# Token groups of 768 and 512 instead of 640 and 640, with weights taken in quarters of a channel pair

## The chip, the cores and the metric

The kernel runs on one core of one Trainium2 chip. The metric is the device time of one execution in microseconds (us); smaller is better. Before the change the median of 3 runs is 2741.11 us (2739.73 to 2746.38). Engines are written as the profile writes them: PE is the matrix engine (its weight loads are PEld), DVE the vector engine, ACT the scalar engine, POOL GpSimd, and SP the engine whose queue issues every DMA of this kernel.

## What is computed

One encoder layer for 1280 tokens (1024 of a prompt and 256 of a sample) of width 2048, in float32:

```
hn   = rmsnorm(x, norm_w)
proj = einsum('btd,dp->btp', hn, w_in)            # 2048 -> 9232 columns
na_q, na_k, na_v, na_g, ml_qk, ml_v, ml_o, ml_z, ml_gp = split(proj)
att  = neighbourhood_attention(na_q, na_k, na_v, rpb) * silu(na_g)      # 8 heads of 128
qk   = silu(centred_depthwise_conv(ml_qk))
h    = rmsnorm(bidirectional_mlstm(mq, mk, ml_v, gates)) # 4 heads of 256
mem  = h * sigmoid(ml_o) * silu(ml_z)
y    = rmsnorm(x + concat(att, mem) @ w_out)             # 2048 -> 2048
```

## The kernel before, in words

A float32 product is made of three matmuls of a rounded type: every operand is split into a high and a low part (ACT casts the high part, DVE subtracts it to get the low part; `split`, L137, and `split_a`, L145), and high x high, high x low and low x high are added in PSUM (`mm_c`, L171). A weight block of 128 x 128 is the stationary operand, tokens are the moving one; for the values (`proj_v`) it is the other way round.

The 1280 tokens are cut into two groups of 640 (`GRP`, L20), and the program has five stages.

1. `first_tiles` (L175) loads group A's activations x, scales and splits them, makes sums and differences of the four blocks that two halves of the 2048 inputs (k tiles 0 to 7 and 8 to 15) and two halves of the tokens (`HALF` = 320) form, keeps them in SBUF (`xb`, `xg`) and computes the first 4 of 56 channel blocks of 128 in the plain way: 384 matmuls of 320 columns. `x_square` and `x_stats` (L117, L124) make the norm's factors.
2. `pair_a` (L236), 34 times: two channel blocks of group A at a time by seven products instead of eight (a 2 x 2 scheme over halves of the inputs and of the tokens). Each half `hf` of the k tiles loads four weight pieces of 128 x 512 (`ra`, 8 buffers), POOL makes four sums of them (`summed`, L278, tile `wt`, 4 buffers), ACT and DVE split the seven weights (`wsa`, 5 buffers), and PE runs 12 matmuls of 320 columns for each: 168 for a pair. In the second half `fold` (L250) adds the seven results from PSUM into `Cn` with eight additions on DVE (L248) and a copy on ACT, and `scaled` (L244) multiplies by the norm's factor. The last 8 pairs are values: PE transposes the result (L310), ACT copies it into `vo` (2 buffers of their own), and it goes to DRAM. `gates_a` (L315) makes the gates between two pairs with 64 matmuls of 320 columns.
3. Group B: for each of 4 heads of the second kind, then 4 pairs of heads of the first kind, `proj_v` (L455) makes the values of 256 columns for the 5 token tiles (30 matmuls of 256 columns in each of 8 steps) and `proj_ch` (L410) one channel block: 16 k tiles x 2 halves of 320 tokens x 3 = 96 matmuls of 320 columns, out of two PSUM banks of the three tagged "pr". Between them the units of both attentions (`na_units`, L524; `ml_units`, L803) are run by `step` (L1052) at a higher priority; the projections fill PE beside them. Three x tiles are loaded ahead (`ahead`, L369) into a pool that outlives group A's.
4. `late_gate` (L436): 24 more `proj_ch` of group B (gates), multiplied into what the units left in `mixT`.
5. The output projection (L1128) for both groups, 1920 matmuls of 512 columns, and the last norm.

The order of instructions on an engine is fixed when the program is built, by a scheduler that takes the ready instruction of highest priority. Tiles of one tag take its buffers in the order of the program: a tile waits for the tile that had its buffer before. DMAs are issued in order by SP.

Of the kernel before, what the change touches and what calls it, by code (L numbers as in the profile page):

```python
# [13 lines left out]
P = 128  # L14
D = 2048
# [3 lines left out]
TT = TS + TP  # L19
GRP = 640  # L20
# [4 lines left out]
HALF = GRP // 2  # L25
NU = 8
VW = 258
NRA, NWS, NWT, NPC = 8, 5, 4, 5
# [6 lines left out]
def kernel(  # L35
# [21 lines left out]
    wp = ctx.enter_context(tc.tile_pool(name="wp", bufs=2))  # L57
# [37 lines left out]
    rbs = [const.tile([P, GRP], F32, tag=f"rstdb{g}", name=f"rstdb{g}") for g in range(2)]  # L95
    rcs = [const.tile([P, 5], F32, tag=f"rstdc{g}", name=f"rstdc{g}") for g in range(2)]
    ssq = [const.tile([P, 5, 4], F32, tag=f"ssq{g}", name=f"ssq{g}") for g in range(2)]
# [5 lines left out]
    def x_raw(g, k, w_):  # L103
        raw = wp.tile([P, GRP], F32, tag="pc", name=f"x{w_}{g}_{k}", bufs=NPC)
        DM.dma_start(raw, xT[g, :, k, :])
        return raw

    def x_split(raw, k, g):
        h = xp.tile([P, GRP], F32R, tag=f"xh{k}", name=f"xh{g}_{k}")
        l = xp.tile([P, GRP], F32R, tag=f"xl{k}", name=f"xl{g}_{k}")  # L110
        S.mul(h, raw, lnw_sb[:, k : k + 1])
# [5 lines left out]
    def x_square(g, i):  # L117
        t, q = divmod(i, 4)
        r0 = (g * 5 + t) * P
        raw = wa.tile([P, 512], F32, tag="ra", name=f"xq{g}_{i}", bufs=NRA)  # L120
        DM.dma_start(raw, xtok[r0 : r0 + P, q * 512 : (q + 1) * 512])
        S.activation(raw, raw, AF.Square, accum_out=ssq[g][:, t, q : q + 1])

    def x_stats(g):  # L124
        rc, rb = rcs[g], rbs[g]
        V.tensor_reduce(rc, ssq[g], axis=mybir.AxisListType.X, op=ALU.add)
        rsqrt_mean(rc, rc, 5, float(D))
        for c, n in ((0, 3), (3, 2)):
            b = bank("a", f"rsps{g}_{c}")
            dg = wp.tile([P, GRP], F32, tag="pc", name=f"xdg{g}_{c}", bufs=NPC)  # L130
            for t in range(n):
                ts_ = slice(t * P, (t + 1) * P)
                V.tensor_scalar(dg[:, ts_], ident, rc[:, c + t : c + t + 1], None, op0=ALU.mult)
            PE.matmul(b[:, : n * P], ones, dg[:, : n * P], start=True, stop=True)
            V.tensor_copy(rb[:, c * P : (c + n) * P], b[:, : n * P])
# [27 lines left out]
    XSLOT = {2: (0, 0), 3: (0, 1), 5: (1, 0), 6: (1, 1), 4: (2, 0), 7: (2, 1)}  # L163
# [10 lines left out]

    def first_tiles():  # L175
        names = ("pr", "pr", "pr", "a", "a", "a", "a", "a")
        pb = [bank(t, f"fb{j}")[:, :HALF] for j, t in enumerate(names)]
        for kk in range(8):
            sc, ws = [], []
            for h in range(2):  # L180
                k = kk + 8 * h
                raw = x_raw(0, k, "r")
                S.mul(raw, raw, lnw_sb[:, k : k + 1])
                sc.append(raw)
                wr = wa.tile([P, 512], F32, tag="ra", name=f"fr{kk}_{h}", bufs=NRA)
                DM.dma_start(
                    wr.rearrange("p (n c) -> p n c", c=P),
                    w_in[0:4, :, k * P : (k + 1) * P].rearrange("n p c -> p n c"),
                )
                t = wa.tile([P, 2, 512], F32R, tag="wsa", name=f"fw{kk}_{h}", bufs=NWS)  # L190
                split_a(t[:, 0], t[:, 1], wr)
                ws.append(t)
            b11, b12 = sc[0][:, :HALF], sc[0][:, HALF:]
            split_a(xb11[kk][:, 0], xb11[kk][:, 1], b11)
            t12 = wa.tile([P, 2, 512], F32R, tag="wsa", name=f"fx{kk}", bufs=NWS)[:, :, :HALF]
            split_a(t12[:, 0], t12[:, 1], b12)
            g0 = xg[0, kk].rearrange("p h c t -> p h (c t)")
# [5 lines left out]
            for h in range(2):  # L203
                for j in range(8):
                    n, c = j // 2, j % 2
                    mm_c(
                        pb[j], lambda a_: ws[h][:, a_, n * P : (n + 1) * P], xs[h, c],
                        kk == 0 and h == 0, kk == 7 and h == 1,
                    )
            tt_ = wp.tile([P, GRP], F32, tag="pc", name=f"ft{kk}", bufs=NPC)  # L210
            V.tensor_tensor(tt_[:, :HALF], b12, b11, op=ALU.subtract)
            V.tensor_tensor(sc[1], sc[1], sc[0], op=ALU.subtract)
            d1, t3 = sc[1][:, :HALF], sc[1][:, HALF:]
            V.tensor_tensor(tt_[:, HALF:], t3, b11, op=ALU.add)
            V.tensor_tensor(d1, d1, t3, op=ALU.subtract)
            for g_, src in ((1, tt_), (2, sc[1])):
                gv = xg[g_, kk].rearrange("p h c t -> p h (c t)")
                split_a(gv[:, 0], gv[:, 1], src)
            if kk > 1:
                for i in range(2 * kk - 4, 2 * kk - 2):  # L220
                    x_square(0, i)
        for i in range(12, 20):
            x_square(0, i)
        Cn = [wp.tile([P, GRP], F32, tag="pc", name=f"fo{n}", bufs=NPC) for n in range(4)]
# [6 lines left out]
        x_stats(0)  # L231
        for n in range(4):
            out_scaled(Cn[n], Cn[n], rbs[0], n)
            DM.dma_start(pT[n][:, 0:GRP], Cn[n])

    def pair_a(n1):  # L236
# [4 lines left out]
        Cn = [wp.tile([P, GRP], F32, tag="pc", name=f"{nm}c{j}", bufs=NPC) for j in range(2)]  # L241
# [27 lines left out]
        for hf in range(2):  # L269
            A = {}  # L270
            for j, f_ in ((0, 0), (1, 0), (1, 1), (0, 1)):
                raw = wa.tile([P, 512], F32, tag="ra", name=f"{nm}r{hf}{j}{f_}", bufs=NRA)
                DM.dma_start(
                    raw, w_in[n1 + j].rearrange("p (h f c) -> p h f c", h=2, f=2)[:, f_, hf, :]
                )
                A[j, f_] = raw

            def summed(i, x, y_, op):  # L278
                t = wa.tile([P, 512], F32, tag="wt", name=f"{nm}t{hf}{i}", bufs=NWT)
                G.tensor_tensor(t, x, y_, op=op)  # L280
                return t

            src = {1: A[0, 0], 4: A[1, 1], 2: A[0, 1]}
            for i in order:
# [8 lines left out]
                t = wa.tile([P, 2, 512], F32R, tag="wsa", name=f"{nm}s{hf}{i}", bufs=NWS)  # L293
# [7 lines left out]
                if hf == 1:  # L301
                    fold(i)
        if n1 < NCH:
            for j in range(2):
                DM.dma_start(pT[n1 + j][:, 0:GRP], Cn[j])
        else:
            for tt in range(5):
# [3 lines left out]
                o = wp.tile([P, 256], F32, tag="vo", name=f"{nm}vo{tt}", bufs=2)  # L311
# [3 lines left out]
    def gates_a():  # L315
        raw = wp.tile([P, GRP], F32, tag="pc", name="gAw", bufs=NPC)[:, :256]
        DM.dma_start(raw, w_g)
        ab = [raw[:, :P], raw[:, P:]]
        sm_ = wa.tile([P, 512], F32, tag="wt", name="gAs", bufs=NWT)[:, :P]
        V.tensor_tensor(sm_, ab[0], ab[1], op=ALU.add)  # L320
        st = []
        ng_ = wa.tile([P, 512], F32, tag="wt", name="gAn", bufs=NWT)[:, :P]
        V.tensor_scalar(ng_, ab[0], -1.0, None, op0=ALU.mult)
        for i, src in enumerate((ab[0], ab[1], sm_, ng_)):
            t = wa.tile([P, 2, 512], F32R, tag="wsa", name=f"gAt{i}", bufs=NWS)
            t = t.rearrange("p h c -> p (h c)")[:, : 8 * 32 + 96]
# [5 lines left out]
        sel = wa.tile([P, 512], F32, tag="wt", name="gAsel", bufs=NWT)  # L332
        V.tensor_tensor(sel[0:32, 0:16], ident[0:32, 0:16], ident[0:32, 16:32], op=ALU.add)
        gs = wp.tile([P, GRP], F32, tag="pc", name="gAg", bufs=NPC)
# [12 lines left out]
        for tt in range(5):  # L347
            b = bank("a", f"gAt{tt}")
            PE.matmul(
                b[:, :16], gs[0:32, tt * P : (tt + 1) * P], sel[0:32, 0:16], start=True, stop=True  # L350
            )
# [14 lines left out]
    ahead = {}  # L366
    for n1 in range(4, NCH + 2 * NU, 2):
        if n1 == NCH + 2 * NU - 2:
            ahead = {k: x_raw(1, k, "r") for k in range(3)}  # L369
# [4 lines left out]
        if 0 <= k < 20:  # L374
            x_square(1, k)
        if k == 20:
            x_stats(1)
# [32 lines left out]
    def proj_ch(g, n, X, late=False):  # L410
        pb = [bank("pr", f"pc{g}_{n}_{c}") for c in range(2)]
        for half in range(2):
            raw = w_piece(w_in[n, :, half * 1024 : (half + 1) * 1024], f"{g}_{n}_{half}")
            for q in range(2):
                t = w_split(raw, q * 512, q * 512 + 512, f"{g}_{n}_{half}_{q}")
                for c in range(2):
                    for kk in range(4):
                        k = half * 8 + q * 4 + kk
                        xh, xl = X.get(k)
                        for wi, xs in ((0, xh), (0, xl), (1, xh)):  # L420
                            PE.matmul(  # L421
                                pb[c][:, :320],
                                t[:, wi, kk * P : (kk + 1) * P],
# [825 lines left out]
```

## Time and profile before

| | |
|---|---|
| median of 3 runs | 2741.11 us |
| the profiled execution | 2743.15 us, of which 2741.1 us are the span from the first to the last instruction |
| mean granted TensorE clock | 0.996 |
| busy in the span | PE 99%, PEld 95%, DVE 64%, ACT 44%, POOL 19% |
| moved by DMA | 380 MB, 139 GB/s in the mean |
| stage 1, first tiles | 8 to 75 us |
| stage 2, the pairs of group A | 75 to 942 us |
| stages 3 and 4, group B | 948 to 2288 us |
| stage 5, output | 2288 to 2741 us |

A busy time is the union of the spans of an engine's instructions. Matmuls are pipelined: one of 320 columns shows a span of 309 ns, while the next starts much earlier. What a matmul costs PE is therefore read from how many of them stand in a stretch in which PE never waits, and not from the mean of one.

### The profile page before, as it was taken

Reading aid. Unit: us, or ns where it says so; the run is one execution under the profiler, and the core shown is the slowest. Engines: PE = TensorE matmul, PEld = TensorE weight load, DVE = VectorE, ACT = ScalarE, POOL = GpSimd, SP = SyncE. Lnnn points to the kernel's source line nnn. Section 1 sums busy time; section 2 is a strip of 40 time slices with the busy share of each in tenths; the row PEclk is TensorE's granted clock in tenths of the full one; section 3 lists DMA queues with packets and bytes.
Section 4 is the critical chain, followed back from the end, with each engine's and each line's share of the span. In section 5 each row is a group of like instructions: output and inputs, shape, how many; then the busy total and the mean of one; then the engine's idle time right before and its main releaser. Section 6 shows DMA issues by size and latency. Waiting matters only on the chain. (4 is left out here: it accounts for less than half of the span.)

```text
span 2741.1 us, 48742 instructions
## 1 busy us (share of the span) xinstructions
PE 2703.6 (99%) x18162; PEld 2611.7 (95%) x18162; DVE 1748.7 (64%) x3681; ACT 1199.7 (44%) x2587; POOL 532.4 (19%) x722
## 2 busy tenths in 40 slices
PE   8999999999999999999999999999999999999998
PEld 7999999999999999999999999999999998887886
DVE  7767667777767667778787786767774334234223
ACT  7333333333334445565565565555553223224222
POOL 1344444444444201101011010000000000111012
PEclk9999999999999999999999999999999999999999
DMA  8334344433333444453444544555554336336334
GB/s 251 99 109 127 115 127 124 129 121 116 117 103 104 136 141 140 124 165 127 137 154 124 158 130 155 170 179 170 180 169 139 106 125 207 100 122 208 100 96 143
DMA packets 220084, 380.09 MB, mean 139 GB/s; under 512 B 22688, under 2 KB 102728, under 8 KB 219720
## 3 DMA queue, kind: packets, MB, share of 16 engines
q1 hardware_dynamic: 219848, 377.00, 43.9%
q8 instruction: 142, 2.33, 0.3%
q14 instruction: 94, 0.77, 0.1%
HBM read 307.14 MB, written 69.77 MB: 138 GB/s over the span
## 5 line engine op out<-in xcount | busy, mean ns | idle before, releaser
L421 PE MATMUL pc<-xh,ws 128*128 128x320 f32 x3584 | 803.8, 307 | 0.8 <-ACT vo L503 0.8
L421 PEld LDWEIGHTS pc<-xh,ws 128*128 128x128 f32 x3584 | 602.0, 188 | 1.2 <-ACT vo L503 1.0
L421 PE MATMUL pc<-xl,ws 128*128 128x320 f32 x1792 | 556.2, 310 | 0.0
L1128 PE MATMUL po<-ws_o,mh 128*128 128x512 f32 x1280 | 399.2, 393 | 1.5 <-DVE ws_o L140 1.5
L421 PEld LDWEIGHTS pc<-xl,ws 128*128 128x128 f32 x1792 | 335.9, 187 | 0.1
L1128 PEld LDWEIGHTS po<-ws_o,mh 128*128 128x128 f32 x1280 | 239.9, 187 | 56.9 <-DVE ws_o L140 2.3
L1128 PE MATMUL po<-ws_o,ml 128*128 128x512 f32 x640 | 249.0, 389 | 0.0
L493 PE MATMUL pv<-wsv,xh 128*128 128x256 f32 (+1 forms) x1280 | 240.4, 285 | 3.9 <-ACT wsv L139 3.9
L139 ACT CAST ws<-wr 128x512 fp32r<-128x512 f32 x224 | 137.7, 616 | 211.7 <-PE pc L421 193.3
L140 DVE TENSOR_TENSOR ws<-wr,ws 128x512 fp32r<-128x512 f32 x224 | 154.3, 690 | 111.9 <-ACT ws L139 108.4
L140 DVE TENSOR_TENSOR ws_o<-wr_o,ws_o 128x512 fp32r<-128x512 f32 x128 | 91.4, 721 | 199.3 <-ACT ws_o L139 199.3
L493 PEld LDWEIGHTS pv<-wsv,xh 128*128 128x128 f32 x1280 | 201.4, 190 | 4.7 <-ACT wsv L139 4.1
L493 PE MATMUL pv<-wsv,xl 128*128 128x256 f32 (+1 forms) x640 | 180.6, 283 | 0.0
L139 ACT CAST ws_o<-wr_o 128x512 fp32r<-128x512 f32 x128 | 77.7, 619 | 214.0 <-PE po L1128 172.1
L1158 POOL TENSOR_TENSOR y<-y,fnb 128x512 f32<-128x512 f32 x40 | 52.7, 1333 | 606.1 <-ACT xr L1157 606.0
L1128 PEld LDWEIGHTS po<-ws_o,ml 128*128 128x128 f32 x640 | 120.1, 188 | 25.8
L493 PEld LDWEIGHTS pv<-wsv,xl 128*128 128x128 f32 x640 | 121.7, 191 | 0.0
L1156 DVE TENSOR_TENSOR y<-po,xr 128x512 f32<-128x512 f32 x40 | 26.8, 687 | 60.7 <-PE po L1128 58.5
L153 DVE TENSOR_TENSOR pco<-pc,rstdb 128x320 f32<-128x320 f32 x96 | 46.6, 485 | 29.5 <-PE pc L421 29.4
L140 DVE TENSOR_TENSOR wsv<-wr_v,wsv 128x256 fp32r<-128x256 f32 x128 | 49.9, 424 | 12.7 <-ACT wsv L139 12.5
L1157 ACT ACTIVATE xr<-y 128x512 f32<-128x512 f32 x40 | 25.1, 628 | 66.2 <-DVE y L1156 61.0
L139 ACT CAST wsv<-wr_v 128x256 fp32r<-128x256 f32 x128 | 45.3, 402 | 16.4 <-PE pv L493 7.2
(1868 smaller groups left out, 5759.1 us busy)
## 6 DMA issues: line engine op xcount, KB each, us to landing
wr<-in_w_in_dram SPq DMA_DIRECT2D x112, 512.0 KB, 4.1
wr_o<-in_w_o_dram SPq DMA_DIRECT2D x64, 512.0 KB, 3.6
wr_v<-in_w_in_dram SPq DMA_DIRECT2D x32, 512.0 KB, 4.1
xr<-in_xT_dram SPq DMA_DIRECT2D x32, 320.0 KB, 5.0
xq<-in_xtok_dram SPq DMA_DIRECT2D x40, 256.0 KB, 3.7
pT<-pco SPq DMA_DIRECT2D x32, 320.0 KB, 2.2
xr<-in_xtok_dram SPq DMA_DIRECT2D x40, 256.0 KB, 3.4
mraw<-mx SPq DMA_DIRECT2D x32, 320.0 KB, 4.3
```

What stands on the lines that cost most here:

```text
L139: S.copy(hi, src)
L140: V.tensor_tensor(lo, src, f(hi), op=ALU.subtract)
L153: V.tensor_tensor(o, src, rb, op=ALU.mult)
L421: PE.matmul(pb[c][:, :320], t[:, wi, kk * P : (kk + 1) * P], xs[:, c * 320 : c * 320 + 320], start=k == 0 and wi == 0 and xs is xh, stop=k ...
L493: PE.matmul(outs[tt], xs[:, tt * P : (tt + 1) * P], t[:, wi, kk * w : (kk + 1) * w], start=k == 0 and wi == 0 and xs is xh and not paired, ...
L1128: PE.matmul(o, xs[:, tt * P : (tt + 1) * P], t[:, wi, :512], start=first and i == 0, stop=last and i == 2,)
L1156: V.tensor_tensor(yt[tt][:, cs], banks[tt], xr, op=ALU.add)
L1157: S.activation(xr, yt[tt][:, cs], AF.Square, accum_out=ss[:, tt, nb : nb + 1])
L1158: G.tensor_tensor(yt[tt][:, cs], yt[tt][:, cs], fnb[:, cs], op=ALU.mult)
```

## The change

Group A has 768 tokens (`GA`, halves of 384) and group B 512 (`GB`).

- First tiles, pairs and gates of group A run the same number of matmuls on 384 columns. `pair_a` loads a quarter of the k tiles of both channel blocks as one piece of 128 x 1024 (`ra`, 3 buffers) and splits and sums in blocks of 128 x 256 (`wsa`, 8 buffers; `wt`, 4): 6 matmuls for each product in a quarter. The copies `vo` of the values (6 for a pair now) use `wt` as well.
- In `first_tiles` the split x12 moves from `wsa` into the ring `pc` (5 buffers), the two sums that had a buffer of their own are made in place, and the squares are taken on 1024 columns.
- `proj_ch` becomes `proj_pair`: two channel blocks, one PSUM bank each, 512 columns for a matmul, 96 matmuls for the two. The weight pieces keep their size.
- `proj_v` has 4 token tiles, out of two "pr" banks instead of three.
- The x tiles of group B are not loaded ahead any more; they come into the new ring `po` (8 buffers) of a pool that takes group A's place, as do the outputs of `proj_pair` and the gates.
- The factors of group B (`x_stats(1)`) are made after group A's end. Both heads of a pair get their projections before the units of the first one. The layouts of w_in and x in DRAM are changed to match; `dynamic_dma_scratch_size` is set to 1024.

```diff
+GA, GB = 768, 512
-HALF = GRP // 2
+HALF = GA // 2
-NRA, NWS, NWT, NPC = 8, 5, 4, 5
+NRA, NWS, NWT, NPC, NPO = 3, 8, 4, 5, 8
...
     def first_tiles():
...
-            t12 = wa.tile([P, 2, 512], F32R, tag="wsa", name=f"fx{kk}", bufs=NWS)[:, :, :HALF]
+            t12 = wa.tile([P, 2, HALF], F32R, tag="pc", name=f"fx{kk}", bufs=NPC)
...
     def pair_a(n1):
...
-        for hf in range(2):
-            A = {}
-            for j, f_ in ((0, 0), (1, 0), (1, 1), (0, 1)):
-                raw = wa.tile([P, 512], F32, tag="ra", name=f"{nm}r{hf}{j}{f_}", bufs=NRA)
...
+        for r in range(4):
+            raw = wa.tile([P, 1024], F32, tag="ra", name=f"{nm}r{r}", bufs=NRA)
+            DM.dma_start(raw, w_in[n1 // 2, r])
+            A = {(j, f_): raw[:, (2 * j + f_) * 256 :][:, :256] for j in range(2) for f_ in range(2)}
...
-                t = wa.tile([P, 512], F32, tag="wt", name=f"{nm}t{hf}{i}", bufs=NWT)
+                t = wa.tile([P, 256], F32, tag="wt", name=f"{nm}t{r}{i}", bufs=NWT)
                 G.tensor_tensor(t, x, y_, op=op)
...
-                for q in range(4):
-                    kk = 4 * hf + q
+                for q in range(2):
+                    kk = 2 * r + q
...
-                if hf == 1:
+                if r == 3:
                     fold(i)
...
-            for tt in range(5):
+            for tt in range(GA // P):
...
-                o = wp.tile([P, 256], F32, tag="vo", name=f"{nm}vo{tt}", bufs=2)
+                o = wa.tile([P, 256], F32, tag="wt", name=f"{nm}vo{tt}", bufs=NWT)
                 S.copy(o, b[:, :256])
...
-    def proj_ch(g, n, X, late=False):
+    def proj_pair(n1, X, late=False):
+        pb = [bank("pr", f"pc{n1}_{j}") for j in range(2)]
+        for r in range(4):
+            raw = w_piece(w_in[n1 // 2, r], f"{n1}_{r}")
+            for j in range(2):
+                t = w_split(raw, j * 512, j * 512 + 512, f"{n1}_{r}{j}")
+                for f_ in range(2):
+                    for q in range(2):
+                        xh, xl = X.get(8 * f_ + 2 * r + q)
+                        c = (2 * f_ + q) * P
                         for wi, xs in ((0, xh), (0, xl), (1, xh)):
                             PE.matmul(
-                                pb[c][:, :320],
+                                pb[j], t[:, wi, c : c + P], xs,
...
-            pb = [bank("pr", f"pv{g}_{u}_{i}") for i in range(3)]
+            pb = [bank("pr", f"pv{u}_{i}") for i in range(nt // 2)]
...
         def get(self, k):
             if k not in self.t:
-                raw = ahead[k] if k in ahead else x_raw(self.g, k, "r")
-                self.t[k] = x_split(raw, k, self.g)
+                self.t[k] = x_split(x_raw(wb, GRP, "po", NPO, 1, k), k, 1)
...
     for u in range(NA_H // 2):
-        proj_v(1, u, X)
+        proj_v(u, X)
+        for n in (QT0 + 2 * u, KT0 + 2 * u):
+            proj_pair(n, X)
         for h in (2 * u, 2 * u + 1):
-            for n in (QT0 + h, KT0 + h):
-                proj_ch(1, n, X)
             for sq in ("p", "s"):
                 run(na_units(sq, h))
```

More of the change, by code (lines that the diff above doesn't have):

```diff
@@ L115, in x_split @@
         return h, l
[L117 to L135, printed above, removed]
     def split(hi, lo, src, scale=None):
@@ L455, in proj_v @@
-    def proj_v(g, u, X):
+                                pb[j], t[:, wi, c : c + P], xs,
+                                start=r == 0 and f_ == 0 and q == 0 and wi == 0 and xs is xh,
+                                stop=r == 3 and f_ == 1 and q == 1 and wi == 1,
+                            )
+        out = []
+        for j in range(2):
+            o = wb.tile([P, GRP], F32, tag="po", name=f"pco{n1}_{j}", bufs=NPO)[:, :GB]
+            out_scaled(o, pb[j], rbs[1], n1)
+            if not late:
+                DM.dma_start(pT[n1 + j][:, GA:], o)
+            out.append(o)
@@ L482, in proj_v @@
                 if gates:
-                    src = graw.rearrange("p (k c) -> p k c", k=4)[:, hp * 2 : hp * 2 + 2, :]
-                    split(t4[:, 0, :, 256:272], t4[:, 1, :, 256:272], src)
-                for tt in range(5):
-                    for kk in range(2):
-                        k = pc * 4 + hp * 2 + kk
-                        xh, xl = X.get(k)
-                        paired = not gates and tt < 4
-                        if k == 0 and paired and tt % 2 == 0:
+                    split(t4[:, 0, :, 256:272], t4[:, 1, :, 256:272], graw[:, f_])
@@ L491, in proj_v @@
+                for tt in range(nt):
+                    for q in range(2):
+                        first, last = r + f_ + q == 0, r == 3 and f_ == 1 and q == 1
+                        xh, xl = X.get(8 * f_ + 2 * r + q)
+                        if first and not gates and tt % 2 == 0:
                             PE.matmul(pb[tt // 2], zer, t[:, 0, :512], start=True, stop=False)
-                        for xs, wi in ((xh, 0), (xh, 1), (xl, 0)):
+                        for m, (xs, wi) in enumerate(((xh, 0), (xh, 1), (xl, 0))):
@@ L495, in proj_v @@
                                 xs[:, tt * P : (tt + 1) * P],
-                                t[:, wi, kk * w : (kk + 1) * w],
-                                start=k == 0 and wi == 0 and xs is xh and not paired,
-                                stop=k == KT - 1 and xs is xl and not (paired and tt % 2 == 0),
-                            )
-        rc = rcs[g]
-        for tt in range(5):
-            o = wp.tile([P, 256], F32, tag="vo", name=f"vo{g}_{u}_{tt}", bufs=2)
+                                t[:, wi, q * w : (q + 1) * w],
+                                start=first and m == 0 and gates,
+                                stop=last and m == 2 and (gates or tt % 2 == 1),
+                            )
+        rc = rcs[1]
+        for tt in range(nt):
+            o = wb.tile([P, 256], F32, tag="vo", name=f"vo{u}_{tt}", bufs=3)
             S.mul(o, outs[tt][:, :256], rc[:, tt : tt + 1])
-            r0 = g * GRP + tt * P
+            r0 = GA + tt * P
             DM.dma_start(vD[u][r0 : r0 + P, :], o)
@@ L1062, in run @@
             step(u_)
[L1064 removed]
+    X = LazyX()
+    rbs[1] = late.tile([P, GB], F32, tag="rstdb1", name="rstdb1")
+    x_stats(1, lambda c: mid(f"xdg1_{c}", 256))
     gates = {}
     for h in range(ML_H):
[L1067 to L1070 removed]
+        proj_v(4 + h, X)
+        for n in (QK0 + 8 + 2 * h, QK0 + 2 * h):
+            proj_pair(n, X)
         for sq in ("p", "s"):
```

285 lines of the change are left out of this document (145 added, 140 removed).

## The prediction

> **What bounds the kernel now.** I read the page first, then stretches of the span (busy time, in brackets the number of instructions, then clock, DMA share, GB/s), because the mean over the span mixes stages.
>
> ```profile
> PE 2703.6 (99%) x18162; PEld 2611.7 (95%) x18162; DVE 1748.7 (64%) x3681; ACT 1199.7 (44%) x2587; POOL 532.4 (19%) x722
> ```
>
> ```profile
> core 0: us, PE busy (x) PEld busy (x) DVE busy (x) ACT busy (x) POOL busy (x), PEclk, DMA share, GB/s
> 8.00:75.00 67.00, 62.73 (x386) 60.82 (x387) 55.76 (x91) 55.62 (x115) 10.43 (x7) 0.97 0.77 236
> 274.00:411.00 137.00, 137.00 (x936) 137.00 (x935) 92.98 (x136) 54.03 (x96) 60.30 (x45) 1.00 0.39 121
> 942.00:980.50 38.50, 34.16 (x251) 33.61 (x251) 23.03 (x48) 22.70 (x51) 4.85 (x27) 0.91 0.70 234
> 948.00:2088.00 1140.00, 1135.32 (x8598) 1130.20 (x8599) 850.67 (x2365) 629.01 (x1549) 87.00 (x347) 1.00 0.49 153
> 2088.00:2288.00 200.00, 200.00 (x1387) 200.00 (x1386) 77.02 (x116) 46.71 (x75) 0.00 (x0) 1.00 0.41 133
> 2590.00:2630.00 40.00, 40.00 (x176) 32.79 (x175) 12.07 (x17) 10.56 (x22) 6.55 (x5) 1.00 0.35 108
> ```
>
> PE waits for almost nothing: it is busy in all of 274 to 411 us (pairs of group A) and in 1135 of the 1140 us in which group B's projections and the attention units share it. So the time is a sum of matmuls, and the change is first a change of that sum. What one costs is read where PE never waits: 137.00 / 936 = 146.4 ns for 320 columns, 40.00 / 176 = 227.3 ns for 512. The 192 columns between them cost 80.9 ns, 0.421 ns each; 384 columns then cost 146.4 + 64 x 0.421 = 173.4 ns. For 256 columns the chain of waits has a run of 18, and it has a long run of 320 as a check:
>
> ```profile
> 1972.96 2.13 PE nap5o L637 x18
> 2088.25 200.24 PE pc L421 x1386
> ```
>
> 2.13 / 18 = 118.3 ns. 200.24 / 1386 = 144.5 ns in the late gates, 1.3% under the 146.4 used here. The intercept is the point: a matmul pays some 12 ns beside its columns, and PE also pays for every column, so fewer, wider matmuls on fewer tokens win and wider ones on more tokens lose.
>
> [...]
>
> **The change, on PE.**
> - Pairs: 34 x 168 = 5712 matmuls from 320 to 384 columns, 27.0 ns each: +154.2 us. First tiles: 384 x 27.0 = +10.4. Gates: 64 x 27.0 = +1.7. Two more transposes for each of 8 value pairs, at no more than the 118 ns above: +1.9.
> - `proj_ch`: 56 x 96 = 5376 x 146.4 = 787.0 us become 28 x 96 = 2688 x 227.3 = 611.0: -176.0.
> - `proj_v`: 8 x 16 x 3 = 384 matmuls of the fifth token tile go: 384 x 118.3 = -45.4.
>
> Together -53.2 us. The output stage keeps its matmuls.
>
> **What hides the rest, and what may not.** The elementwise rows:
>
> ```profile
> L147 DVE TENSOR_TENSOR A22s<-A22t,A22s 128x512 fp32r<-128x512 f32 x8 | 6.0, 747 | 4.8 <-ACT A22s L146 4.8
> L280 POOL TENSOR_TENSOR A22t<-A22r,A22r 128x512 f32<-128x512 f32 x4 | 5.4, 1347 | 8.5 <-DVE A22s L147 6.0 <-DVE A20s L147 2.6
> L248 DVE TENSOR_TENSOR A22c<-A22c,A22b 128x320 f32<-128x320 f32 x7 | 3.3, 480 | 0.4 <-PE A22b L173 0.4
> L911 POOL TENSOR_TENSOR mlp_1dm<-mlp_1al,mask_f x8: 460/704/1087, 1075.1 to 1587.1; 128x128 f32<-128x128 f32 x8
> L153 DVE TENSOR_TENSOR pco<-pc,rstdb 128x320 f32<-128x320 f32 x96 | 46.6, 485 | 29.5 <-PE pc L421 29.4
> L140 DVE TENSOR_TENSOR wsv<-wr_v,wsv 128x256 fp32r<-128x256 f32 x128 | 49.9, 424 | 12.7 <-ACT wsv L139 12.5
> L139 ACT CAST wsv<-wr_v 128x256 fp32r<-128x256 f32 x128 | 45.3, 402 | 16.4 <-PE pv L493 7.2
> ```
>
> *Quarters in a pair.* A pair lasts 168 x 173.4 = 29.1 us. ACT: 28 casts x 0.402 = 11.3. DVE: 28 x 0.424 = 11.9, twelve folds and scalings of 384 columns at about 0.56 = 6.7. POOL: 16 sums of 256; between 1347 / 2 = 674 ns and the line from 460 (128 columns) to 1347 (512), 756; I take 756: 12.1. Each has room. PE idle from it: 0 to 75 us (the first rival), I take 3.
>
> *First tiles.* ACT and DVE were busy 55.6 and 55.8 of 67 us; with 1.2 times the columns 67, and PE's stretch becomes 77. But x12 now waits in `pc` for the buffer of the step before, until its last split. 0 to 8 us, I take 2.
>
> *Value copies in the ring of the sums.* The pair's own profile around its end:
>
> ```profile
> 919.53 1.48 POOL L280 TENSOR_TENSOR A70t<-A70r,A70r 128x512 f32<-128x512 f32 x1 [3.23 <-DVE A70s L147]
> 919.77 1.78 DVE L147 TENSOR_TENSOR A70s<-A70r,A70s 128x512 fp32r<-128x512 f32 x1
> 921.17 0.60 PE L310 MATMUL A68v<-ident,A68c 128*128 128x128 f32 x4
> 923.79 0.86 ACT L312 COPY A68vo<-A68v 128x256 f32<-128x256 f32 x2 [1.03 <-DMA vD<-A68vo]
> 942.12 0.49 DVE L248 TENSOR_TENSOR A70c<-A70c,A70b 128x320 f32<-128x320 f32 x1
> 944.30 0.62 ACT L312 COPY A70vo<-A70v 128x256 f32<-128x256 f32 x2
> vD<-vo SPq DMA_DIRECT2D x40, 128.0 KB, 1.8
> ```
>
> The third copy waited for a write-out, because its two buffers were taken. With `wt` the first sum of the next pair (for product 5) takes the buffer of the third copy and must wait for that copy's write-out. At the last pair the copies began 2.2 us after the last fold began. So: 2.2 + 0.3 + issue 0.4 + 1.8 landing + sum 0.76 + split 0.83 = 6.3 us from a pair's end to product 5. PE has meanwhile products 1, 4 and 2 of this quarter and 1 of the next, which need no sum: 4 x 6 x 0.173 = 4.2, and 12 transposes, 1.3: 0.8 us short; if it has only product 1, 4.0. Seven such ends: 6 to 28 us. I take 2 x 7 = 14, since the order can be rearranged only in part. Behind the waiting sum on POOL stand only the other sums.
>
> *From A to B.*
>
> ```profile
> 942.12 2.27 ACT L111 ACTIVATE xh<-xr,lnw_sb 128x640 fp32r<-128x640 f32 x3 [8.14 <-PE A70b L173]
> 946.43 1.32 ACT L139 CAST wsv<-wr_v 128x256 fp32r<-128x256 f32 x4 [1.51 <-DMA wr_v<-in_w_in_dram]
> 947.92 1.12 PE L493 MATMUL pv<-wsv,xh 128*128 128x272 f32 x3 [3.86 <-ACT wsv L139]
> wr_v<-in_w_in_dram SPq DMA_DIRECT2D x32, 512.0 KB, 4.1
> xr<-in_xT_dram SPq DMA_DIRECT2D x32, 320.0 KB, 5.0
> ```
>
> Everything in group A's place waits for its last matmul. Three x tiles were there already; now a quarter's weights (0.5 MB) and four x tiles (1.05 MB) must come: 1.55 MB at the 234 GB/s of that stretch is 6.6 us, with splits 8 to 9 against 5.8 before. -2 (the stretch also had 4 us of other idle time) to +10, I take +4.
>
> *Group B.* The weight splits stay as many; 112 scalings of 320 become 56 of 512. DVE's share rises, since PE's work shrinks beside it: of the 56 channel blocks 200 / (96 x 0.1444) = 14.4 were left at 2088 us, so some 42 were done, and PE saves 42 x 3.14 + 45 = 177, DVE 42 x (2 x 0.485 - 0.747) = 9: 842 of 963 us, 87% after 75%. PE may wait now and then: 0 to 42 us (second rival), I take 6. `proj_v` no longer takes all three "pr" banks: 0 to -9, I take -2.
>
> Sum: -53.2 + 3 + 2 + 14 + 4 + 6 - 2 = -26 us. The profiled execution took 2743.15 us, 2.05 over its span of 2741.1; the median of the runs is 2741.11, so I set the sum against 2741.1: **2715 us**, 1.0% faster.
>
> **The rivals.**
>
> *DVE and POOL fall behind in the last quarter: slower.* All folds now fall into a quarter of 42 x 0.173 = 7.3 us instead of a half of 84 x 0.146 = 12.3. Two rows above show the cause of alarm: a sum on POOL at 919.53 and a DVE split at 919.77 that took 1.78 us instead of 0.75. Added without overlap the last quarter asks for 4 sums 3.0, 7 splits 3.0, 12 folds and scalings 6.7: 12.7 us, 5.4 too many. What covers that are weights split ahead: 7 products x 1.04 = 7.3 us if all eight buffers are full. Before: 4 x 1.35 + 7 x 0.75 + 12 x 0.48 = 16.4 against 12.3, 4.1 too many, covered by 4 x 1.76 = 7.0, and PE showed no idle time. If only three products are ahead (3.1 us), each of 34 pairs loses 2.3 us: 78 - 3 on the forecast, **2790 us**. It decides from fewer than five products ahead. Against: the additions from PSUM kept 480 ns with sums beside them. [...]
>
> *The attention units set group B's end: no change.* They ended at 2088, 1140 us after group B's start, while PE's work in group B, 1140 + 200 us, becomes 1340 - 221 = 1119. At their old pace they end 21 us after PE's work; 2% slower, for DVE's 87%, 44. Forecast + 36 = **2751 us**. Against it:
>
> ```profile
> 2080.13 0.35 DVE L602 TENSOR_SCALAR nas_1st<-nas_1st,nas_1sm 128x256 f32<-128x256 f32 x1
> 2083.39 0.38 PE L616 MATMUL nas_1t<-ident,nas_1st 128*128 128x128 f32 x2
> ```
>
> The unit was ready at 2080.5 and waited 2.9 us while PE ran projections ahead of it in its order: the units follow PE, and get faster with it.
>
> *Everything is hidden: faster still.* The order is rearranged so that value copies, transition and DVE cost nothing: 2741.1 - 53.2 - 2 = **2686 us**.
>
> **How the numbers follow.** Forecast 0.56, DVE and POOL 0.14, units 0.11, all hidden 0.19. A measurement of this kernel can tell about 0.3% (8 us) from no change. Faster: 0.53 of the forecast's 0.56 and 0.19: 0.72. Same: 0.03 and 0.08 of the units' 0.11: 0.11. Slower: 0.14 and 0.03: 0.17. The forecast's own range, all its costs at their low or high ends without the two rivals, is 2683 to 2743. From 2680, a little under the case in which all is hidden, to 2757, a little over that of the units, is left out hardly more than the DVE rival's 0.14: that is the range.
>
> **What would show it.** In the new profile: 137 us of a steady pair holds about 790 matmuls (173.4 ns); a pair lasts 29.1 us; `proj_pair` groups show 227 ns in the late gates; idle PE of about 2 us behind each value pair, released by a split whose sum waited for vD<-vo; 8 to 9 us between A and B. PE idle in every pair with DVE at 90% would show the first rival; PE idle at the end of group B with units still running, the second. I am wrong on the main term if 384 columns cost more than 183 ns, which makes the pairs eat the whole gain.

## The result, and the profile after

The changed kernel is slower: 2816.55 us, median of 4 runs (2815.01 to 2818.4), against 2740.42 us for the kernel before in the same comparison; ratio 1.0275, 95% interval 1.0256 to 1.0294. The forecast was 2715 us. The profiled execution has a span of 2816.0 us. One of the five runs of a kernel further down (value copies, statistics and eight buffers together) took 3020.94 us with its clock at 0.827 and is left out of that kernel's median.

The first lines to read are again the total of the engines and then the stages. The first fence is from the page of the changed kernel, the second is its busy time by stretch (columns as before: busy time of PE, PEld, DVE, ACT and POOL with the number of instructions, the granted clock, the DMA share, GB/s). The stretches are the first tiles, some five pairs from the middle of group A, one value pair, the transition from A to B, group B while it has projections, group B after its last projection, and the output.

```profile
PE 2699.5 (96%) x15108; PEld 2477.6 (88%) x15108; DVE 1838.9 (65%) x4117; ACT 1287.6 (46%) x3023; POOL 590.0 (21%) x994
```

```profile
8.00:83.50 75.50, 70.53 (x384) 69.02 (x384) 59.63 (x107) 59.75 (x112) 0.91 (x2) 1.00 0.70 219
300.00:437.00 137.00, 137.00 (x793) 137.00 (x792) 97.43 (x189) 58.85 (x146) 60.47 (x78) 1.00 0.37 118
961.80:999.20 37.40, 32.89 (x181) 31.78 (x181) 22.14 (x40) 13.51 (x35) 13.04 (x16) 0.95 0.25 78
1149.70:1170.80 21.10, 3.85 (x17) 2.58 (x17) 15.83 (x34) 12.65 (x30) 4.74 (x27) 0.60 0.94 320
1170.80:2237.00 1066.20, 1064.56 (x6375) 943.97 (x6373) 811.56 (x2126) 594.14 (x1421) 82.73 (x323) 1.00 0.51 159
2237.00:2364.00 127.00, 86.48 (x538) 78.54 (x537) 96.18 (x289) 69.30 (x167) 4.16 (x24) 0.81 0.55 172
2364.00:2806.00 442.00, 440.55 (x1924) 359.90 (x1924) 143.55 (x207) 126.76 (x237) 60.81 (x57) 1.00 0.42 135
```

PE is busy 96% of a longer span, after 99%. Where it is not busy, the stretches are easy to see: the value pairs (32.89 of 37.40), the transition (3.85 of 21.10) and the end of group B (86.48 of 127.00). In all three the clock is under 1.00 too (0.95, 0.60 and 0.81). In the steady pairs PE has no idle time, and in the stretch with projections 1.6 us.

Set against the prediction's own terms, stage by stage (us; the last column is the last kernel of the experiments below):

| stage | before | by the prediction's terms | after | last kernel |
|---|---|---|---|---|
| to the first matmul of the pairs | 74.8 | 87.2 | 83.5 | 83.7 |
| 26 pairs and the gates | 660.3 | 782.2 | 774.7 | 774.5 |
| 8 value pairs, to their last product | 207.0 | 259.9 | 291.5 | 243.0 |
| from there to the first matmul of group B | 5.8 | 9.8 | 21.1 | 6.1 |
| group B, to the first output matmul | 1340.4 | 1123.0 | 1193.0 | 1140.7 |
| output, to the end | 452.8 | 452.8 | 452.2 | 453.4 |
| span | 2741.1 | 2714.9 | 2816.0 | 2701.4 |

The first two rows and the last are right within 8 us. The miss of 101 us lies in three places, 32 in the value pairs, 11 in the transition and 70 in group B, less 12 by which the other rows came in under their terms. The longest waits of PE over the whole span name the same three, and the first tiles (`fb`), where the kernel before has 12.1 us of the same wait; columns are the waiting instruction, what released it, us in total, times, longest.

```profile
PE nap_0t L625 <- DVE nap_0st L611: 13.7, 3, 5.1
PE rsps L133 <- DMA wr_v<-in_w_in_dram: 13.2, 1, 13.2
PE fb L181 <- ACT xb L154: 10.3, 3, 8.1
...
PE A68b L181 <- ACT A68s L154: 4.3, 1, 4.3
...
PE A60b L181 <- ACT A60s L154: 3.5, 1, 3.5
```

At one end of a value pair the order of events (start, length, engine, line, operation; in brackets the idle time before and what ended it) is:

```profile
961.81 1.21 PE L181 MATMUL A62b<-xb,A62s 128*128 128x384 f32 x6
...
964.01 1.73 PE L330 MATMUL A60v<-ident,A60c 128*128 128x128 f32 x12 [1.00 <-DVE A60c L161]
...
966.96 0.86 ACT L332 COPY A60vo<-A60v 128x256 f32<-128x256 f32 x2 [1.01 <-DMA vD<-A60vo]
968.00 0.72 POOL L300 TENSOR_TENSOR A62t<-A62r 128x256 f32<-128x256 f32 x1 [19.80 <-DMA vD<-A60vo]
968.76 0.41 ACT L154 CAST A62s<-A62t 128x256 fp32r<-128x256 f32 x1 [0.94 <-POOL A62t L300]
...
969.22 6.07 PE L181 MATMUL A62b<-xg,A62s 128*128 128x384 f32 x23 [3.48 <-ACT A62s L154]
```

This is the wait that the prediction described: POOL's first sum for the next pair waits for the write-out of a value copy, its split follows, and PE, which has run product 1 only, stands for 3.48 us. What remains is its size, and the two other places.

### The profile page after: what moved, and what is told of

Its sections match the earlier page's. It is cut to its first block, busy times and chain, and to the rows that moved or that the text cites. A ratio compares the mean times of both kernels' runs of the same rounds, so it can differ in the third digit from the quotient of the medians.

```text
span 2816.0 us, 44070 instructions
## 1 busy us (share of the span) xinstructions
PE 2699.5 (96%) x15108; PEld 2477.6 (88%) x15108; DVE 1838.9 (65%) x4117; ACT 1287.6 (46%) x3023; POOL 590.0 (21%) x994
## 4 chain that ended last, share of the span: by engine, by line
PE 85%; DMA 5%; DVE 5%; ACT 2%; issue 1%; POOL 0%; SPq 0%; ACTq 0%; POOLq 0%; DVEq 0%
PE pc L434 19%; PE po L1140 15%; PE pv L502 6%; PE A4b L181 1%; PE A70b L181 1%; PE A8b L181 1%; PE A54b L181 1%; PE A52b L181 1%; PE A50b L181 1%; PE A48b L181 1%; PE A44b L181 1%; PE A42b L181 1%; PE A40b L181 1%; PE A38b L181 1%; PE A36b L181 1%
## 5 line engine op out<-in xcount | busy, mean ns | idle before, releaser
L434 PE MATMUL pc<-xh,ws 128*128 128x512 f32 x1792 | 573.9, 396 | 0.0
L434 PEld LDWEIGHTS pc<-xh,ws 128*128 128x128 f32 x1792 | 335.3, 189 | 66.2
L434 PE MATMUL pc<-xl,ws 128*128 128x512 f32 x896 | 355.6, 397 | 0.0
L434 PEld LDWEIGHTS pc<-xl,ws 128*128 128x128 f32 x896 | 168.3, 188 | 33.5
L502 PE MATMUL pv<-wsv,xh 128*128 128x256 f32 (+1 forms) x1024 | 191.4, 284 | 0.0
L502 PEld LDWEIGHTS pv<-wsv,xh 128*128 128x128 f32 x1024 | 160.9, 190 | 1.3 <-DVE wsv L148 0.4
L502 PE MATMUL pv<-wsv,xl 128*128 128x256 f32 (+1 forms) x512 | 144.8, 283 | 0.0
L502 PEld LDWEIGHTS pv<-wsv,xl 128*128 128x128 f32 x512 | 97.3, 190 | 0.0
L148 DVE TENSOR_TENSOR ml<-mraw,mh 128x640 fp32r<-128x640 f32 x32 | 27.0, 850 | 25.2 <-ACT mh L147 25.1
```

Of the source, the lines that this page charges most:

```text
L148: V.tensor_tensor(lo, src, f(hi), op=ALU.subtract)
L434: PE.matmul(pb[j], t[:, wi, c : c + P], xs, start=r == 0 and f_ == 0 and q == 0 and wi == 0 and xs is xh, stop=r == 3 and f_ == 1 and q == ...
L502: PE.matmul(outs[tt], xs[:, tt * P : (tt + 1) * P], t[:, wi, q * w : (q + 1) * w], start=first and m == 0 and gates, stop=last and m == 2 ...
```

## The experiments

### The value copies in buffers of their own

```diff
-                o = wa.tile([P, 256], F32, tag="wt", name=f"{nm}vo{tt}", bufs=NWT)
+                o = wa.tile([P, 256], F32, tag="vo", name=f"{nm}vo{tt}", bufs=2)
```

> The six value copies of a value pair get two buffers of their own, as before the change, in place of the ring of the weight sums; nothing else is edited. Theory (ring of the sums): the first sum of the next pair no longer waits 19.8 us for the write-out of a copy, product 5 follows product 1, and a value pair falls from 37.2-38.0 us to 30-32 us (29.1 and the transposes): 7 boundaries x 6 to 8 us = 42 to 57 us less, 2760 to 2775 us; the clock in the value pairs returns to 1.00. Rival (quarters run the ring of split weights empty at each value pair's end, whatever the copies do): value pairs stay above 36 us and the time at 2805 to 2817.

Measured: 2775.0 us, 41.5 less than the changed kernel (ratio to the kernel before 1.0125, interval 1.0109 to 1.0142). The value pairs take 30.4 us each in the mean, 48 us less for the eight. One value pair of this kernel:

```profile
947.00:977.80 30.80, 30.79 (x182) 30.32 (x181) 20.68 (x41) 13.09 (x35) 12.22 (x16) 1.00 0.30 95
```

PE is busy in all of it and the clock is 1.00: 29.1 us of products and 1.3 of transposes, nothing else. The theory holds, the rival falls. In the profiled executions the span falls by 44.5 us: 48.4 in the value pairs, less 4.2 because the transition that follows became longer (25.3 in place of 21.1) and 2.2 in the output, with 2.5 won elsewhere.

### The statistics of group B behind the first value projection

The change had moved `x_stats(1)` from the middle of group A to the place right behind its end. In PE's order its two matmuls `rsps` stand ahead of the first `pv`, and their operand `xdg` is made on DVE at 1168.5 us, behind ten splits of x tiles that start between 1156.3 and 1167.7, in a transition whose DMA share is 0.94 (320 GB/s).

```diff
-    x_stats(1, lambda c: mid(f"xdg1_{c}", 256))
...
         proj_v(4 + h, X)
+        if h == 0:
+            x_stats(1, lambda c: mid(f"xdg1_{c}", 256))
```

> The statistics of group B (two small matmuls rsps) are issued after the first value projection, which does not need them, in place of ahead of it. Theory (order on PE): the first pv matmul starts at about 1158 in place of 1170.8, since its operands were there by 1157; 9 to 12 us less, 2804 to 2808. Rival (the x tiles, which are no longer fetched ahead): at 340 GB/s the queue is full until 1171, PE waits for x tiles instead, and 0 to 4 us are won: 2812 to 2817.

Measured: 2804.79 us, 11.8 less (ratio 1.0233, 1.0218 to 1.0248). The timeline of the changed kernel, and then of this one:

```profile
1168.51 1.03 DVE L130 TENSOR_SCALAR xdg<-ident,rstdc 128x128 f32<-128x128 f32 x4
...
1169.31 2.05 PE L133 MATMUL rsps<-xdg,ones 128*128 128x256 f32 x4 [13.23 <-DMA wr_v<-in_w_in_dram]
...
1170.80 1.01 PE L502 MATMUL pv<-wsv,xh 128*128 128x272 f32 x2
```

```profile
1156.35 0.69 PE L330 MATMUL A70v<-ident,A70c 128*128 128x128 f32 x2 [1.84 <-ACT A70vo L332]
1157.24 1.73 PE L502 MATMUL pv<-wsv,xh 128*128 128x272 f32 x6 [0.21 <-ACT xh L139]
```

The first `pv` starts 6.5 us after group A's last product, close to the 5.8 of the kernel before, although no x tile is fetched ahead. So the 13.2 us were an order on PE, and the transfers that the prediction charged cost almost nothing: `pv` takes a quarter of the k tiles at a time, and from 1148 to 1190 us PE waited for its operands once, 0.2 us. The releaser that the wait row names (wr_v) was of no help; the row of `xdg` just ahead of it was.

### Group B: who sets its end

The changed kernel's projections end at 2237, and for the 127 us up to the first output matmul the units of attention run alone, with PE busy two thirds of the time. That is the sight that the prediction gave for its second rival. The question is why: have the units a pace of their own, or does PE's order hand them their time badly? Three edits of the order and of the load came first.

*The gates that wait for units come first.*

```diff
-    for ch in range(0, 8, 2):
-        late_gate(OT0 + ch, 8 + ch, X)
...
     for h in range(0, NA_H, 2):
         late_gate(GT0 + h, h, X)
+    for ch in range(0, 8, 2):
+        late_gate(OT0 + ch, 8 + ch, X)
```

> The late gates change places: those of the neighbourhood heads, which must wait for their units, come ahead of the eight output-gate pairs, which need no unit that is still running. Theory (the order in which PE is given projections: the late gates ran ahead of the units, took PE from them until 2237 and left 127 us with nothing beside the units): projections last to the end of group B, PE stays busy, group B falls from 1193 to 1130-1150 us: 45 to 65 us less, 2752 to 2772. Rival (the units have a pace of their own, set by their chain over DVE, ACT and transfers, and end at about 2364 whatever runs beside them): the last three or four pairs of projections come after that, 65 to 87 us more, 2880 to 2900.

Measured: 2868.04 us, 51.5 more (ratio 1.0464, 1.0448 to 1.0479). The stretch of the neighbourhood heads, and the rest of the projections behind them (to 2418 us, then the first output matmuls):

```profile
1929.00:2344.00 415.00, 339.22 (x1940) 296.14 (x1939) 288.48 (x821) 206.53 (x481) 12.76 (x68) 0.90 0.50 158
2344.00:2440.00 96.00, 96.00 (x422) 78.66 (x421) 48.84 (x73) 37.34 (x61) 0.00 (x0) 1.00 0.60 205
```

The last matmul of the units came only 14 us earlier (2355 in place of 2369), and more than four pairs of projections were left for the time from the start of the last head on: the rival's picture, though 12 us short of its range. But PE was idle for 76 of the 415 us. In five of the first seven heads it had one pair of projections (96 to 105 matmuls), in the other two none. As the program is written, a gate of a neighbourhood head holds buffers of `po` until that head is done, and the gates behind it wait for them; that this is what left PE without work was not tried. The edit made a new shortage; it doesn't decide.

*No late gates.* Edit: both loops of `late_gate` are taken out.

> Left out: all late gates (12 pairs of projections, 1152 matmuls of 512 columns, 262 us of PE, with their gating), so the gated columns of group B go ungated into the output. Theory (units follow PE, and get faster where less is ahead of them): the neighbourhood heads take 37 us each, as in the stretch without projections, 170 to 250 us less, 2570 to 2650. Rival (own pace of the units): they end 0 to 60 us earlier than 2364, 2755 to 2817.

Measured: 2678.12 us, 138 less, between the two. Two stretches of neighbourhood heads alone (three, the first of them still beside the last units of the other kind, and five):

```profile
1912.00:2040.00 128.00, 81.75 (x532) 72.67 (x532) 96.73 (x312) 73.07 (x180) 7.18 (x30) 0.85 0.50 154
2040.00:2224.00 184.00, 127.20 (x799) 114.46 (x800) 139.74 (x429) 103.61 (x244) 7.03 (x40) 0.83 0.52 161
```

Without projections a head takes 35 to 38 us, as the theory had it, and PE is busy in two thirds of that, at a clock of 0.83 to 0.85. So the units are slowed by what stands beside them; a fixed pace of 48 or 60 us is not theirs. The first three heads of the second kind, ahead of this, stayed at 173 to 179 us; the neighbourhood heads start 14 us earlier after the start of group B, and 125 of the 139 us by which group B is shorter come from them.

*Gates of both kinds in turn.*

```diff
-    for ch in range(0, 8, 2):
-        late_gate(OT0 + ch, 8 + ch, X)
...
     for h in range(0, NA_H, 2):
         late_gate(GT0 + h, h, X)
...
+        late_gate(OT0 + h, 8 + h, X)
```

> The late gates alternate: one pair of a neighbourhood gate, which waits for its units, then the two pairs of an output gate, four times over. In PE's order 19.3, 20.5, 21.9, 23.5, 24.6, 26.4, 27.4 and 28.0 pairs of projections then stand ahead of the eight neighbourhood heads, in place of 19.3, 21.3, 23.1, 25.1, 26.9 and three times 28.0. Theory (beside projections PE is the bound, and the loss is PE's idle time where none are left): a head costs 20 us of its own matmuls and 21.8 a pair, at least 36: 370 us for the eight heads where the same sum gives 398 for the changed kernel; 20 to 35 us less, 2782 to 2797. Rival (the units have a pace of their own that any projections disturb: heads took 36 us with no pair beside them, about 52 with one and 60 with two in the runs so far, so that spreading the pairs thin costs): the same sum by these three figures is 412 in place of 398; 8 to 20 us more, 2825 to 2837.

Measured: 2838.54 us, 22 more (ratio 1.0351, 1.0337 to 1.0366). This is the rival's side, just over its range. PE is idle by turns, in heads beside which fewer projections stand:

```profile
2000.00:2050.00 50.00, 40.26 (x222) 35.49 (x221) 37.36 (x99) 25.22 (x57) 1.38 (x8) 0.86 0.53 165
2050.00:2110.00 60.00, 60.00 (x336) 51.95 (x336) 38.24 (x100) 28.13 (x62) 1.39 (x8) 1.00 0.54 172
```

So spreading whole pairs over the heads is no remedy. A head is slow while a pair runs (60 us) and PE idles when none may (9.7 of 50 us).

### The three remedies so far, together

> Two edits together: the value copies' own two buffers, and group B's statistics behind the first value projection. Theory (two separate losses): they add, 41.5 + 11.8 us less, 2761 to 2765; with the transition 4 us longer after the first edit alone, which the second mends, down to 2757. Rival (group B's end is set by the units' chain from a fixed point, so that an earlier start is given back there): 2775 or more.

Measured: 2759.12 us (ratio 1.0062, 1.0049 to 1.0076): 57.4 less, the 53 of the sum and the 4 of the transition. By stages, the value pairs won 49 us and the transition, now 6.7 us, won 14: two separate losses. Group B gave back 6 us of them (1198.7), which it did after neither edit alone; that stays open.

The next two have eight buffers of `mid`, the ring of bias tables, scores and raw tiles of the units, in place of six (`bufs=6` in `mid`): alone, and with the two edits above.

> The attention units' ring mid has eight buffers in place of six; nothing else is edited. Theory (the units are slow because bias tables, scores and the next head's raw tiles share six buffers, so that loads start late): units get ahead of the projections, heads without projections take about 30 us in place of 36, and the stretch without projections shrinks by a head or more: 20 to 45 us less, 2772 to 2797. Rival (the units' pace is set by the hand-over from engine to engine, and not by buffers): within 8 us of 2816.5.

> All three edits together: value copies in their own two buffers, statistics behind the first value projection, eight buffers of mid. By the sum of the three: 2763 less what the eight buffers bring. If that is 20 to 45 us, 2718 to 2743, at or under the kernel before (2740.7); if it is nothing, 2755 to 2765, still 0.6 to 0.9% slower than before.

Measured: 2805.55 us alone, 11 less (1.0231, 1.0215 to 1.0246), half of the least that the theory expected and 3 more than the rival allowed; heads beside projections still take 61 to 65 us, and those without 38. All three together: 2755.86 us (ratio 1.0051, 1.0037 to 1.0065), 3.3 less than without the eight buffers, which is within the spread of the runs. Buffers were not what set the pace of the neighbourhood heads.

### The width of the projections

What a head has beside it can be counted. This is the busy time of `proj_ch` on PE (columns: PE, PEld, clock, DMA share, GB/s) from the start of one neighbourhood head to the start of the next, in the kernel before, and then of `proj_pair` in the changed one:

```profile
1840.40:1886.80 46.40, 31.25 (x187) 27.53 (x186) 1.00 0.56 180
1886.80:1935.40 48.60, 33.62 (x199) 29.54 (x200) 1.00 0.56 175
1935.40:1983.30 47.90, 33.44 (x198) 29.14 (x197) 1.00 0.59 183
```

```profile
2069.90:2133.20 63.30, 47.84 (x192) 34.60 (x191) 1.00 0.54 173
2133.20:2194.60 61.40, 46.20 (x183) 32.91 (x182) 1.00 0.55 182
2194.60:2248.20 53.60, 32.41 (x127) 22.64 (x125) 0.95 0.61 198
```

The order that was fixed when the program was built holds about 190 projection matmuls for a head in both kernels (the heads next to these have 217 and 197 before, 170 after; in the last row the projections run out). Before they had 320 columns, now they have 512. 192 x 80.9 ns (the prediction's difference of the two prices) is 15.5 us: a head of 48 us becomes one of 63. And since there are half as many of them, they are used up during the fifth head. The slow heads are not the loss themselves, for PE never waits in them. Counted from the start of one matmul to the start of the next, the head's own matmuls take 18 to 19 us in both kernels and the projections the rest. The loss comes behind them, in the end of the fifth head and the last three, which have no projections left: 40.5 us of idle PE, and a clock of 0.81. That makes a third theory, and a test in which PE's work grows:

```diff
-                            PE.matmul(
-                                pb[j], t[:, wi, c : c + P], xs,
...
+                            wd = GB if first or last else 256
+                            for h_ in range(0, GB, wd):
+                                PE.matmul(
+                                    pb[j][:, h_ : h_ + wd], t[:, wi, c : c + P],
+                                    xs[:, h_ : h_ + wd], start=first, stop=last,
+                                )
```

> Group B's projections as two 256-wide matmuls in place of one 512-wide one (but for the first and the last of each sum); PE's work in group B grows by 28 pairs x 0.86 us = 24 us, and nothing else is edited. Theory (PE's order holds about 192 projection matmuls beside each neighbourhood head, before the change and after it, whatever their width: 192 x 146 ns = 28 us before, 192 x 227 = 44 after, so that the heads are slowed and the projections run out four heads early): with 240 to 290 matmuls of 118 ns a head, 28 to 34 us, heads take 48 to 55 us each to the last but one, PE stays busy, and group B falls from 1193 to about 1169 although PE has more to do: 2785 to 2800. Rival (the units are slowed by what their chain needs on DVE, ACT and the queues, where the width of PE's matmuls changes nothing): nothing is won and the 24 us come on top, 2816 to 2842.

Measured: 2783.14 us, 33.4 less (ratio 1.0152, 1.0135 to 1.0169) and 2 under the theory's range, though PE has more to do: 18 us, counted from start to start, where 24 were reckoned. Group B takes 1156.2 us. Its stretch up to the last head, and the last head:

```profile
1171.90:2282.00 1110.10, 1109.91 (x9216) 1102.45 (x9215) 863.62 (x2313) 634.22 (x1525) 86.43 (x339) 1.00 0.51 164
2282.00:2328.00 46.00, 38.25 (x272) 34.99 (x271) 38.24 (x104) 28.46 (x66) 1.41 (x8) 0.93 0.66 215
```

PE is never idle in the first 1110 us. The rival, by which the width changes nothing, is out by 33 us at the least.

In the changed kernel only the late gates run beside the neighbourhood heads, so only they need to be narrow. The last kernel has the three edits and halves for the late gates alone:

```diff
-                            wd = GB if first or last else 256
+                            wd = GB if first or last or not late else 256
```

> The three edits together (value copies in their own buffers, statistics behind the first value projection, eight buffers of mid), and the late gates' projections, which are those beside the neighbourhood heads, as two 256-wide matmuls; the others stay 512 wide. Theory (too many microseconds of projections in PE's order beside each head): heads of 46 to 52 us with projections beside them to the end, no stretch without, group B from 1192 to about 1140: 2700 to 2715. Rival (the width of PE's matmuls changes nothing): 2756 to 2768.

Measured: 2702.69 us (2702.23 to 2706.22); ratio to the kernel before 0.9861, interval 0.9847 to 0.9876, and 53.2 us less than the same kernel with 512 columns everywhere. From head to head, and group B as a whole:

```profile
1943.90:1995.10 51.20, 36.75 (x263) 33.23 (x262) 1.00 0.61 190
1995.10:2044.00 48.90, 33.88 (x248) 30.82 (x247) 1.00 0.58 189
2044.00:2090.40 46.40, 31.86 (x228) 28.72 (x227) 1.00 0.52 167
```

```profile
1107.30:2248.00 1140.70, 1138.25 (x8020) 1066.35 (x8021) 909.89 (x2427) 665.26 (x1602) 92.40 (x361) 1.00 0.52 170
```

A head has 32 to 37 us of projections beside it, as in the kernel before, takes 46 to 51 us, and the projections last to the end of group B: PE is busy in 1138 of 1141 us. This kernel is 1.4% faster than the one before.

Where PE's time in group B goes, in us, counted from the start of each matmul to the start of the next with idle time taken out:

| | before | after | last kernel |
|---|---|---|---|
| projections of channel blocks | 790.6 | 627.7 | 638.4 |
| projections of values | 236.4 | 190.2 | 191.0 |
| the units' matmuls | 308.7 | 333.0 | 308.9 |
| PE idle | 4.7 | 42.1 | 2.4 |
| together | 1340.4 | 1193.0 | 1140.7 |

The units do the same work in all three. In the changed kernel it cost 24 us more, all of it behind the last projection, where the clock is 0.81. The last kernel has that back, and the idle time.

## Why the prediction was wrong, point by point

**The sum of matmuls was right in group A and 13 us too good in group B.** 137 us of steady pairs hold 793 matmuls, 172.8 ns each, where 790 and 173.4 were forecast; a pair takes 29.1 us. The 26 pairs with the gates grew by 114.4 us against 121.9, the first tiles by 8.7 against 12.4. In group B the channel blocks went from 790.6 to 627.7 us, 162.9 less where 176.0 were forecast: a matmul of 512 columns took 233.5 ns there (627.7 / 2688), and not the 227.3 that were read in the output stage; one of 320 took 147.1, close to the 146.4 that were reckoned. The values gave 46.2 against 45.4.

**The first rival did not come.** DVE is busy 97.43 of 137.00 us in the steady pairs and POOL 60.47, and PE does not wait. Single instructions do take longer beside each other: a split's subtraction of 256 columns takes between 411 and 962 ns in those pairs (never more than 427 where no sum runs beside it), and a sum of 256 on POOL 732 to 989 (never more than 742 where no split runs beside it). It cost nothing there, since no wait of PE came of it.

**The step "value copies in the ring of the sums" had the right cause and too small a size.** It said 6 to 28 us, 14 taken, 0.8 to 4.0 us at each of seven ends; the edit that removes it gives back 48 us, 7 at each end. The trace splits these: 3.48 us of waiting for the split, at the upper end of what was reckoned, because PE ran only product 1 ahead and not products 4 and 2; 1.00 for the last scaling ahead of the transposes, which was not reckoned at all; and some 2 because PE comes back slower (below). The choice of a value "since the order can be rearranged only in part" had no row behind it. Even the upper end, 28, was too low by 20, because it left out the last two of these.

**The step "From A to B" left out what the change had moved.** It priced transfers, with 8 to 9 us as the sum. `x_stats(1)` had been in the middle of group A, where nothing waited for it, and was now the first thing that PE did in group B; its matmuls and its DVE work were given no price. They were the 13.2 us. The transfers that were priced were hidden.

**The second rival happened, and was argued away by one row.** The row showed a unit that was ready and waited 2.9 us while PE ran projections ahead of it. It was right that units wait for PE's order. The step from there to "get faster with it" was wrong: it holds only if the projections ahead of each unit get shorter, and they got longer, 234 in place of 147 ns each with about as many of them. The rival's own price, 36 us on the forecast (40 by its figures, 44 in place of +6 and -2), was too small as well, because it kept the units' old pace. In the profile after, the heads behind the first take 58 to 63 us beside projections and, once these are used up, 35 to 41 us with PE two thirds busy and its clock at 0.81. What was added to the sum for PE's waits in group B was 6 us. The runs showed 62: 37 of idle PE and 24 more for the units' matmuls, in the stretch with the clock at 0.81. These 56 too few and the 13 of the matmuls' price are the miss of 70 in group B but for 1.

What is shown and what is not: that the width of the projections sets the pace of the heads is shown by the two runs with halves, each a single edit from its neighbour. That the order takes about as many matmuls for a head whatever their width is only a count in these kernels; with halves it took some 230 to 280, not 190. Why it takes so many was not tried. The halves also cut PE's work into finer pieces for whatever fixes the order; the runs cannot tell this from the width itself. Eight buffers of `mid` alone brought 11 us and next to the other edits 3.3; that difference stays open.

## What to carry to other kernels

Work that fills the gaps of a chain sets the chain's pace. When its instructions grow, count how many of them stand between two steps of the chain in the order on that engine, multiply by the new duration, and check that they last to the chain's end: the loss is what comes after the last of them. When a tile moves into another tag's ring, find the first tile that gets its buffer next and follow that tile to the engine that sets the time; charge the upper end unless a row shows what fills the wait. Of a step that a change moves, price every instruction on every in-order engine that it now stands ahead of, even where it is two matmuls.

## What the runs showed of the hardware that was not expected

In the value pairs a wait of PE cost more than its length. These are the two stretches after the 3.48 us of idle time in the value pair shown above:

```profile
969.20:973.50 4.30, 4.25 (x14) 3.93 (x15) 4.11 (x6) 2.95 (x8) 4.22 (x6) 0.60 0.00 0
973.50:977.50 4.00, 4.00 (x25) 4.00 (x24) 4.00 (x7) 1.63 (x4) 2.85 (x4) 1.00 0.45 135
```

For 4.3 us the granted clock is 0.60 and 14 matmuls take 4.25 us, 304 ns each, where the steady pairs need 173: 1.8 us on top of the wait. All seven ends show it, with waits of 3.4 to 4.3 us and then a granted clock of 0.50 for 3.4 us. In the value pair with the copies in buffers of their own, where PE is busy in 30.79 of 30.80 us, the clock is 1.00. The same loss shows in the stretch without projections at the end of group B, behind a shorter wait. The clock is at 0.50 from 2243.0 to 2249.8 us, and from 2239.6 to 2243.0 PE was busy for 1.1 us and its longest wait took 2.1. No wait in that stretch is longer than 5.1 us; PE is busy in 86.48 of its 127.00 us, and the mean clock is 0.81.
